# Hybrid decoder layer on one core: out-projection of four pairs of column tiles by seven products of blocks, and x added to the residual by adding transfers

## The chip, the cores and the metric

The kernel runs on one core of a Trainium2 chip. The metric is the device time of one execution in microseconds (us); a time given for a kernel is the median of its runs. The core's engines are PE (matrix products), DVE, ACT and POOL (elementwise work), and SP, which here issues nearly all transfers. Each engine works through its own instructions in order and waits for the others by semaphores.

## The reference

One decoder layer over 16 meta tokens and 512 tokens (528 positions), width 2048, all in float32:

```python
n = rmsnorm(h, g_pre_mix)
z = n @ w_in                                       # 2048 x 6592
y_conv = short_conv_group(z[..., :CONV_COLS], conv_w)
y_rwkv = rwkv7_group(z[..., CONV_COLS:], ...)      # a scan over the positions, 16 heads of 64
mix = concatenate([y_conv, y_rwkv], axis=-1) @ w_out   # 2048 x 2048, the out-projection
h = h + rmsnorm(mix, g_post_mix)                   # the first residual
f = conv_glu(rmsnorm(h, g_pre_ffn), w_gate_up, conv_ffn, w_down)   # FFN, 2048 -> 2 x 5632 -> 2048
h = h + rmsnorm(f, g_post_ffn)
return h[:, N_META:]
```

The change is in the line with `w_out` and in the first residual.

## The kernel before, in words

**Numbers.** Every float32 value is split into a high and a low part (ACT casts to get `hi`, DVE subtracts to get `lo`), and a product is three matmuls: hi by hi, hi by lo, lo by hi. Activations lie with the width on the partitions, in tiles of 128 rows by the positions; the 514 positions that are needed from the out-projection on are worked in two halves, `HY` = (0, 258) and (258, 514).

**Out-projection.** There are 16 column tiles `m` of 128 output rows. Each takes 4 weight blocks of 128x512 (`wload`: SP loads `raw`, which has 3 buffers; ACT casts `whi`, DVE subtracts `wlo`) and runs 16 row tiles k x 3 matmuls x 2 halves = 96 matmuls into one PSUM tile (`mps` or `u`). The 16 activation tiles `ys` are the outputs of the scan and of the convolution. Twelve of them come back from the DRAM tensor `ysp` through `r` and `v`, four are still on the chip, and all are split into `ahi` and `alo` just before the projection. `mixed` takes each result: ACT squares it (`q`), POOL adds the square into the sum `hxh` (the code's `ss`), and ACT copies it times a gain into `acc` (the code's `h`).

**Last two tiles, and the residual.** Column tiles 14 and 15 keep their split weights (`tt`), run half 0 of both and then half 1 of both, so that the norm and the residual of half 0 go beside the matmuls of half 1. The norm sums `hxh` and `q` over the partitions by matmuls with ones (`psn`) and ends in `r1p`. `residual(i)` then works through half i in 8 steps of two row tiles: DVE multiplies `acc` by `r1p`, x (which SP has loaded into a `raw` buffer) is added, by DVE and POOL in turn, and each row tile is split into activations for the FFN (`tt`, then `ahi` and `alo`). The second half also writes h to the DRAM tensor `hsp`.

**FFN.** The first two column blocks go by plain products, half 0 ahead of half 1. Later blocks go by `seven`: seven products of 2x2 blocks in place of eight, on sums of weight blocks and of activation blocks. Weights come as blocks `R` of 128x1024 (5 buffers); ACT casts `H`, DVE subtracts `O`.

**Order.** While `plan.on` holds, instructions are kept back, and a planner orders them with its own table of costs (0.42 us for an issue on SP, a latency for a landing, and so on). It is on from column tile `M0 = 10` to the end. Ahead of that, the order is the one in which the tile framework issues. All instructions that the planner has handled show one source line in the profile, L220, so that what follows goes by tile names.

```python
                (G if m % 4 else V).tensor_tensor(out=x, in0=x, in1=xr, op=ALU.add)
        for m in range(KT - 2):
            plan.on = m >= M0
```

Of the kernel before, what the change touches and what calls it, by code (L numbers as in the profile page):

```python
# [10 lines left out]
F32 = mybir.dt.float32  # L11
# [7 lines left out]
D = 2048  # L19
SEQ = 512  # L20
# [59 lines left out]

M0 = 10

# [141 lines left out]
class Plan:  # L224
# [3 lines left out]
    def __init__(self, tc):  # L228
        self.tc, self.on, self.kept, self.stage, self.rank, self.pe_rank = tc, False, [], 0, 2, 2

    @contextmanager
# [44 lines left out]
    def time(self, x):  # L276
# [46 lines left out]
    def land(self, x, issued):  # L323

        a = x["out"] if isinstance(x["out"], View) and x["out"].tile.pool.space != "dram" else x["ins"][0]
        n = a.parts * 4
        for s in a.ids.shape[1:]:
            n *= s
        self.pipe = max(self.pipe, issued) + n / 230e3
        return self.pipe + LAND + (2.0 if a.parts in (C, 4 * NC) else 0)  # L330

# [35 lines left out]
    def lag(self, u, v):  # L367

        e = self.engine[u]
        return 0.0 if e == self.engine[v] != "SP" else HOP[e]  # L370
# [44 lines left out]
    def run(self, rank):  # L415
# [10 lines left out]
        for _ in units:  # L426
# [31 lines left out]
            free[e], busy[e] = start + d, (start + d, self.two(x))  # L458
            end = self.land(x, start + d) if e == "SP" else start + d + (0.22 if e == "PE" else 0)
            for v in self.after[u]:  # L460
                o = self.engine[v]
                ready[v] = max(ready[v], start + d if o == e != "SP" else end + 0.07 + GAP[o])
# [17 lines left out]
def hymba(tc, I, out, ysp=None):  # L480
# [26 lines left out]
    if ysp is None:  # L507
        ysp = dp.tile([KT, 128, TY], F32, name="ysp")

    def wload(src, into=None):  # L510
# [27 lines left out]
    def run(g):  # L538
        for _ in g:
            pass  # L540
# [50 lines left out]
    with ExitStack() as ctx1:  # L591
# [455 lines left out]
        def head_norm(P, tags):  # L1047
# [41 lines left out]
            else:  # L1089
                o = p1.tile([128, LP], F32, name="k", bufs=2)[:, T0:L]  # L1090
                V.scalar_tensor_tensor(out=o, in0=yc[:, T0:], scalar=pc("lnb", P), in1=g[:, T0:], op0=ALU.add,
                                       op1=ALU.mult)
                ylast[NP + P] = o

        ylast = {}
        HC = ((T0 - 2, T0 - 2 + 258), (T0 + 256, L))

        def conv(j):
# [14 lines left out]
            (G if j < NP - 1 else V).tensor_tensor(out=u, in0=u, in1=zb, op=ALU.mult)  # L1113
            if j < NP - 1:
                SP.dma_start(ysp[j], u)
            else:
                ylast[j] = u
# [36 lines left out]
        while tasks or any(fills) or cur:  # L1154
# [32 lines left out]
            try:  # L1187
# [5 lines left out]
                cur = None  # L1193
        ys = []
        for i, k in enumerate(KORD):
            if k in ylast:
                yr = ylast[k]
            else:
                yr = p1.tile([128, LP], F32, name="rv"[i % 2], bufs=2)[:, :TY]
                SP.dma_start(yr, ysp[k])  # L1200
            hi, lo = a_tiles(i, TY)
            split(yr, hi, lo)
            ys.append((hi, lo))
        plan.give()


    with ExitStack() as ctx2:
# [42 lines left out]

        def mixed(ps, m, i):
            a, b = HY[i]
            x = ps[i][:, :b - a]
            sq[i] = ss[i] if m == 0 else small(b - a)
# [6 lines left out]
        def residual(i):  # L1261
# [26 lines left out]

        for m in range(KT - 2):
            plan.on = m >= M0  # L1290
            t = mp.tile([128, 2, 512], F32, name="mps")
            ps = [t[:, i] for i in range(2)]
            run(fill(gemm(I["w_out"][m], ys, [half(ps, i)[0] for i in range(2)])))
            for i in range(2):
                mixed(ps, m, i)

        H = KT // 2
# [3 lines left out]

        b11 = block(2)
        last = []
        for n, m in enumerate(range(KT - 2, KT)):
            kw = p2.tile([128, KT // 4, 2, 512], F32R, name=f"tt{n}", bufs=1)
            keep = [(kw[:, ku, 0], kw[:, ku, 1]) for ku in range(KT // 4)]
            if n == 0:
                ps = [ps2.tile([128, 512], F32, name="u", bufs=2) for _ in range(2)]  # L1310
            else:
                t = mp.tile([128, 2, 512], F32, name="mps")
                ps = [t[:, i] for i in range(2)]
            run(fill(gemm(I["w_out"][m], ys, half(ps, 0), into=keep)))
            mixed(ps, m, 0)
            last.append((ps, keep))
        n = 0
        res = iter(())
        for m, (ps, keep) in zip(range(KT - 2, KT), last):
            for _ in fill(gemm(None, ys, half(ps, 1), kept=keep)):  # L1320
                n += 1
                if n == N1:
                    rms1(0)
                    res = residual(0)
                if n % 4 == 0:
                    next(res, None)
            mixed(ps, m, 1)
        run(res)


        rb = wide("rb")
        rw = [rb[:, i * HW:i * HW + 258] for i in range(2)]

# [5 lines left out]
        def parted(raw, hi=None, lo=None):  # L1339
# [14 lines left out]
            return lambda c: at(hi, c), lambda c: at(lo, c)  # L1354

        def standard(outs, w, m0, x, first, last):
# [106 lines left out]

        def less(o, x, y):
            V.tensor_tensor(out=o, in0=x, in1=y, op=ALU.subtract)

        def sums(X2, X3):
# [68 lines left out]
        run(su)  # L1536


        X11 = [act(j, 0) for j in range(H)]
# [4 lines left out]
        X4 = [[x[:, :258] for x in hs[j]] for j in range(H)]  # L1544

        acc = p2.tile([128, KT, SEQ], F32, name="acc", bufs=1)

# [8 lines left out]
        def seven(f):  # L1556
# [15 lines left out]
            def plus(o, x, y):  # L1572
                V.tensor_tensor(out=o, in0=x, in1=y, op=ALU.add)

# [256 lines left out]
def layout(np, inp):  # L1831
# [20 lines left out]
    r["w_in"] = tiles(np.concatenate(cols, axis=1))  # L1852
    r["w_out"] = tiles(A["w_out"].reshape(KT, 128, D)[list(KORD)].reshape(D, D))

# [49 lines left out]
```

## Time and profile before

| | us |
|---|---|
| median of three runs (2397.4 to 2397.72) | 2397.53 |
| profiled execution, its own time | 2395.92 |
| its span, first to last instruction | 2394.1 |
| PE busy, 98% of the span | 2354.7 |
| DVE busy, 71% | 1699.1 |
| ACT busy, 50% | 1202.7 |
| POOL busy, 26% | 632.0 |

The mean granted TensorE clock was 0.996. The out-projection starts near 797 us and its last matmul is at about 981 us; the FFN follows. In tables by stretch, each line gives the stretch, its length, then the busy time and number of instructions of PE, PE's weight loads, DVE, ACT and POOL, then the granted clock, the busy share of the transfer engines, and GB/s. In tables of groups, each line has the count, the busy time and the mean in ns, and then the idle time before them with what ended it. In timelines, a line has the start, the duration, the instruction, and in brackets the idle time before it with its releaser.

### The profile page before, as it was taken

The numbers are of one execution on the slowest core, as the hardware profiler recorded it, in microseconds if no ns is written. First come the engines' busy times: TensorE is split into PE (matmuls) and PEld (weight loads), VectorE is DVE, ScalarE is ACT, GpSimd is POOL, SyncE is SP. The second block draws the span as 40 slices with busy tenths as digits, with TensorE's granted clock in tenths as the row PEclk, the third lists the DMA queues.
The fourth block names the chain that finished last, engine by engine and source line by source line (L and its number), as shares of the span: only waits on it lengthen the run. The fifth ranks groups of instructions, "written<-read, shape, count | busy, mean of one in ns | idle before, by whom it ended". The sixth has DMA issues, their size and how long they took to land.

```text
span 2394.1 us, 46253 instructions
## 1 busy us (share of the span) xinstructions
PE 2354.7 (98%) x18546; PEld 2249.2 (94%) x18546; DVE 1699.1 (71%) x2277; ACT 1202.7 (50%) x2364; POOL 632.0 (26%) x734
## 2 busy tenths in 40 slices
PE   7999999999999999999999999999999999999996
PEld 7999999999999999998999999999999998989896
DVE  7678888888764523785768677776868686859586
ACT  7766766767654434564434334343434342525254
POOL 2222646555451011210212121111212121202025
PEclk9999999999999999999999999999999999999998
DMA  5444333333432435523332324242324242423352
GB/s 178 151 132 121 89 92 89 105 107 95 130 103 85 133 93 176 177 76 106 96 116 80 124 80 133 80 124 81 123 74 130 71 134 79 124 88 107 96 191 71
DMA packets 130103, 265.53 MB, mean 111 GB/s; under 512 B 29888, under 2 KB 42944, under 8 KB 129888
## 3 DMA queue, kind: packets, MB, share of 16 engines
q1 hardware_dynamic: 129888, 262.57, 35.5%
q8 instruction: 146, 2.39, 0.4%
q14 instruction: 69, 0.57, 0.1%
HBM read 239.57 MB, written 22.95 MB: 110 GB/s over the span
## 4 chain that ended last, share of the span: by engine, by line
PE 56%; DVE 2%; issue 0%; ACT 0%; POOL 0%; ACTq 0%; DVEq 0%; POOLq 0%
PE mps L220 30%; PE u L220 16%; PE d L220 10%; DVE acc L220 1%; DVE alo L220 0%; DVE raw L220 0%; PE psn L220 0%; DVE q L220 0%; POOL raw L220 0%; ACT q L220 0%; DVE O L220 0%; DVE tt L220 0%; ACT raw L220 0%; ACT acc L220 0%; DVE r1p L220 0%
## 5 line engine op out<-in xcount | busy, mean ns | idle before, releaser
L220 ACT CAST H<-R 128x1024 fp32r<-128x1024 f32 x373 | 391.2, 1050 | 454.0 <-PE u L220 179.1
L220 DVE TENSOR_TENSOR O<-R,H 128x1024 fp32r<-128x1024 f32 x373 | 487.0, 1306 | 108.3 <-ACT H L220 107.5
L220 PE MATMUL mps<-ahi,whi 128*128 128x264 f32 (+2 forms) x2080 | 416.7, 288 | 10.5 <-ACT whi L220 10.5
L220 PE MATMUL mps<-alo,whi 128*128 128x264 f32 (+2 forms) x2080 | 416.0, 288 | 0.7 <-DVE alo L220 0.7
L220 PE MATMUL mps<-ahi,wlo 128*128 128x264 f32 (+2 forms) x2080 | 412.7, 287 | 1.6 <-DVE wlo L220 1.6
L220 DVE TENSOR_TENSOR wlo<-raw,whi 128x512 fp32r<-128x512 f32 x293 | 221.1, 758 | 208.1 <-ACT whi L220 189.0
L220 PEld LDWEIGHTS mps<-ahi,whi 128*128 128x128 f32 x2080 | 318.1, 189 | 13.2 <-ACT whi L220 10.7
L220 PEld LDWEIGHTS mps<-alo,whi 128*128 128x128 f32 x2080 | 317.6, 189 | 3.5 <-DVE alo L220 1.1
L220 PEld LDWEIGHTS mps<-ahi,wlo 128*128 128x128 f32 x2080 | 317.4, 190 | 3.8 <-DVE wlo L220 1.8
L220 ACT CAST whi<-raw 128x512 fp32r<-128x512 f32 x293 | 180.2, 619 | 195.9 <-PE mps L220 152.6
L220 POOL TENSOR_TENSOR raw<-raw,rb 128x516 f32<-128x516 f32 (+1 forms) x45 | 91.7, 2039 | 669.1 <-DVE raw L220 614.3
L220 PE MATMUL mps<-tt,H 128*128 128x258 f32 x1968 | 263.6, 284 | 1.3 <-DVE tt L220 1.3
L220 PE MATMUL mps<-alo,H 128*128 128x258 f32 x1032 | 253.7, 283 | 0.7 <-DVE alo L220 0.5
L220 PE MATMUL mps<-ahi,H 128*128 128x258 f32 x1032 | 253.4, 282 | 0.4 <-ACT ahi L220 0.4
L220 PEld LDWEIGHTS mps<-tt,H 128*128 128x128 f32 x1968 | 250.1, 189 | 2.4 <-DVE tt L220 1.6
L220 POOL TENSOR_TENSOR R<-R 128x1024 f32<-128x1024 f32 x40 | 131.4, 3286 | 422.6 <-DVE R L220 400.1
L220 DVE TENSOR_TENSOR R<-R 128x1024 f32<-128x1024 f32 x120 | 206.5, 1721 | 1.1
L220 PEld LDWEIGHTS mps<-ahi,H 128*128 128x128 f32 x1032 | 194.5, 190 | 0.6 <-ACT ahi L220 0.6
L220 PEld LDWEIGHTS mps<-alo,H 128*128 128x128 f32 x1032 | 193.9, 189 | 1.1 <-DVE alo L220 1.1
L220 POOL TENSOR_SCALAR SUV<-VT 32x64 f32<-32x64 f32 x272 | 138.0, 508 | 159.3 <-PE st L220 132.6
L220 PE MATMUL mps<-ahi,O 128*128 128x258 f32 x1032 | 152.5, 283 | 0.0
L220 PE MATMUL mps<-tt,O 128*128 128x258 f32 x984 | 141.1, 282 | 0.0
(318 smaller groups left out, 4409.1 us busy)
## 6 DMA issues: line engine op xcount, KB each, us to landing
R<-w_gu_dram SPq DMA_DIRECT2D x176, 512.0 KB, 3.6
raw<-w_in_dram SPq DMA_DIRECT2D x208, 256.0 KB, 2.7
R<-w_down_dram SPq DMA_DIRECT2D x88, 512.0 KB, 4.4
raw<-w_out_dram SPq DMA_DIRECT2D x64, 256.0 KB, 2.6
l<-lo SPq DMA_DIRECT2D x24, 264.0 KB, 2.3
hsp<-acc SPq DMA_DIRECT2D x8, 512.0 KB, 5.7
tt<-hsp SPq DMA_DIRECT2D x4, 1024.0 KB, 11.7
lo<-l SPq DMA_DIRECT2D x12, 264.0 KB, 2.8
```

The source lines that it names most:

```text
L220: return getattr(self.real, op)(*real, **{k: x.get() if isinstance(x, View) else x for k, x in kw.items()})
```

## The change

It has three parts.

**Seven products.** Column tiles 0 to 5 (`MS = 6`), 14 and 15 stay as they were. Tiles 6 to 13 become four pairs. A pair is a 2x2 arrangement of weight blocks (two row halves of 1024 by two columns of 128) against a 2x2 arrangement of activations (two row halves by the two halves of the positions). It takes 7 products of 8 row tiles x 3 matmuls of 258 columns. Its weights are four `R` blocks of 512 KB from a new tensor `w_pair`; DVE builds four sums of 128x1024 (`R<-R`) and the low parts of seven blocks. The sums of activations `T2`, `T3`, `T4` are built by `sums` during tiles 2 to 5 from 16 more reloads of `ysp`, and a fourth set, `Y1`, is written over half of the old activations by `again` (8 reloads). What it overwrites, half 1 of eight tiles, is written to a DRAM tensor `y12` ahead of that (16 writes of 128x256) and read back for tiles 14 and 15 (16 reads). Four `ylast` tiles are now also written to `ysp`.

**Residual.** SP's loads of x are gone, and so are the additions on POOL and DVE. POOL issues 16 transfers that add x from DRAM to `acc`.

**Order.** The planner is on from column tile 2 (`MP = 2`) and knows of transfers on POOL's queue: 0.9 us for the issue, 2.0 us more until it lands. `JS` sets how many `sums` stand ahead of which tile.

```diff
-M0 = 10
+MS = 6
+MP, JS, HEAD = 2, (0, 0, 3, 3, 2, 0), 8.0
...
         if e == "POOL":
+            if op == "dma_start":
+                return 0.9
...
+        return self.pipe + LAND + (2.0 if a.parts in (C, 4 * NC) or x["engine"].name == "POOL" else 0)
...
+        free["PE"] = self.head
...
             for m in range(0, KT, 2):
-                xr = wide().rearrange("p (m t) -> p m t", m=2)[:, :, :b - a]
-                SP.dma_start(xr, I["xT"][m:m + 2, :, T0 + a:T0 + b].rearrange("m p t -> p m t"))
-                x = h[:, m:m + 2, a:b]
+                x, src = h[:, m:m + 2, a:b], I["xT"][m:m + 2, :, T0 + a:T0 + b].rearrange("m p t -> p m t")
                 V.tensor_tensor(out=x, in0=x, in1=r1[i].unsqueeze(1).to_broadcast([128, 2, b - a]), op=ALU.mult)
-                (G if m % 4 else V).tensor_tensor(out=x, in0=x, in1=xr, op=ALU.add)
+                G.dma_start(x, src, accum_op=ALU.add)
...
+        def sums(j):
+            y = [big("R", F32)[:, :TY] for _ in range(2)]
+            for x, k in zip(y, (j, H + j)):
+                SP.dma_start(x, ysp[KORD[k]])
+            t = two()
+            less(t[:, 0], y[1][:, 256:], y[0][:, 256:])
+            plus(t[:, 1], t[:, 0], y[0][:, :258])
+            x = y[1][:, :258]
+            less(x, x, t[:, 1])
+            for o, x in ((T2, t[:, 1]), (T3, t[:, 0]), (T4, x)):
+                split(x, o[:, j, 0], o[:, j, 1])
...
-        for m in range(KT - 2):
-            plan.on = m >= M0
+        for m in range(MS):
+            plan.on = m >= MP
+            for _ in range(JS[m]):
+                sums(next(left))
...
+            if m == 1:
+                for x, o in zip(yf[:H], y12):
+                    for i in range(2):
+                        SP.dma_start(o[i], x[i][:, 258:TY].bitcast(F32))
...
+        for j in range(H):
+            y = again(j, wide()[:, :TY])
+            less(y[:, :258], y[:, 256:], y[:, :258])
+            split(y[:, :258], *[x[:, HA:HA + 258] for x in yf[j]])
...
+        def product(raw, x, o=None, start=True):
+            o = ps2.tile([128, 512], F32, name="u", bufs=2)[:, :258] if o is None else o
+            w = parted(raw)
+            for p, q in ((0, 0), (0, 1), (1, 0)):
+                with plan.step(2, FILL):
+                    for j in range(H):
+                        PE.matmul(o, w[p](128 * j), x[j][q], start=(start and p == q == j == 0), stop=p == 1 and j == H - 1,
+                                  skip_group_check=True)
+            return o
+
+        def pair(n):
+            a22, a21, a11, a12 = (load(I["w_pair"][n, i]) for i in (3, 2, 0, 1))
+            s1 = big("R", F32)
+            plus(s1, a21, a22)
+            k = two()
...
+            c = product(a11, Y11, mp.tile([128, 2, 512], F32, name="mps")[:, 0, :258])
+            S.copy(k[:, 0], c)
+            row(0, 0, product(a12, Y21), k[:, 0])
+            less(a11, s1, a11)
+            product(a11, Y2, c, False)
+            S.copy(k[:, 1], c)
+            less(a21, a22, a11)
+            less(a11, a12, a11)
+            plus(k[:, 1], product(a11, Y22), k[:, 1])
+            product(a21, Y3, c, False)
+            S.copy(k[:, 0], c)
+            product(a22, Y4, c, False)
+            row(1, 0, c)
+            o = product(s1, Y1)
+            row(0, 1, o, k[:, 1])
+            row(1, 1, o, k[:, 0])
+
+        for n in range((KT - 2 - MS) // 2):
+            pair(n)
...
+        for j in range(H):
+            for x, o in zip(yf[j], y12[j]):
+                SP.dma_start(x[:, 258:TY].bitcast(F32), o)
```

In program order, PE's matmuls go from 17593 to 17497: 384 of 256 columns leave and 288 of 258 columns are added. Three places in the order matter.

First, SP's queue at the start of the out-projection. Before, with `w_in` the end of the projection ahead, `w_out` the weights, and `r` and `v` the reloads of `ysp`:

```order
L220 DMA raw<-w_in_dram 128x512 x6
L220 DMA raw<-w_out_dram 128x512
L220 DMA r<-ysp 128x514
L220 DMA v<-ysp 128x514
L220 DMA r<-ysp 128x514
L220 DMA raw<-w_out_dram 128x512
L220 DMA v<-ysp 128x514
L220 DMA raw<-w_out_dram 128x512
L220 DMA r<-ysp 128x514
L220 DMA v<-ysp 128x514
```

And after:

```order
L223 DMA raw<-w_in_dram 128x512 x6
L223 DMA y_11765<-ahi_11275 128x256
L223 DMA raw<-w_out_dram 128x512
L223 DMA r<-ysp 128x514
L223 DMA y_11765<-alo_11287 128x256
L223 DMA v<-ysp 128x514
L223 DMA y_11765<-ahi_11291 128x256
L223 DMA y_11765<-alo_11301 128x256
L223 DMA r<-ysp 128x514
L223 DMA y_11765<-ahi_11309 128x256
L223 DMA raw<-w_out_dram 128x512
L223 DMA v<-ysp 128x514
```

The writes of `y12` now stand between the loads of the tiles and of the first weights; 13 of the 16 are ahead of the last `r`.

Second, POOL and DVE at the residual. POOL before:

```order
L220 TENSOR_TENSOR hxh<-hxh,q 128x258
L220 TENSOR_TENSOR acc<-acc,raw 128x2x258
L220 TENSOR_TENSOR hxh<-hxh,q 128x256
L220 TENSOR_TENSOR acc<-acc,raw 128x2x258 x3
L220 TENSOR_TENSOR acc<-acc,raw 128x2x256 x4
```

POOL after:

```order
L223 TENSOR_TENSOR hxh<-hxh,q 128x258
L223 DMA acc<-xT_dram 128x2x258 x2
L223 TENSOR_TENSOR hxh<-hxh,q 128x256
L223 DMA acc<-xT_dram 128x2x258 x6
L223 DMA acc<-xT_dram 128x2x256 x8
```

DVE after, from the norm of half 0 to the last multiplications of half 1:

```order
L223 TENSOR_TENSOR acc<-acc,r1p 128x2x258 x8
L223 TENSOR_TENSOR tt_13681<-R,tt_13681 128x1024 x2
L223 SCALAR_TENSOR_TENSOR tt_13738<-acc,par,tt_13738 128x258
L223 TENSOR_SCALAR q<-psn 128x256
L223 SCALAR_TENSOR_TENSOR tt_13738<-acc,par,tt_13738 128x258 x3
L223 TENSOR_TENSOR q<-q 128x256
L223 TENSOR_SCALAR q<-q 128x256
L223 TENSOR_TENSOR r1p<-hxl,q 128x256
L223 SCALAR_TENSOR_TENSOR tt_13738<-acc,par,tt_13738 128x258 x4
```

After these follow six low parts `alo` of half 0, three multiplications of half 1, two `alo` and the other five multiplications. Before, DVE's multiplications and additions alternated with the splits; now all eight multiplications of half 0 go first, and all additions are transfers on POOL's queue, half 1's behind half 0's.

Third, ACT at the start of the FFN, where `tt` with `acc` is the high part of an FFN activation and `q<-mps`, `acc<-mps` are the square and the copy of the last column tile's half 1. Before:

```order
L220 ACTIVATE q<-u 128x256
L220 CAST tt_13568<-R 128x1024
L220 ACTIVATE tt_13584<-acc,par 128x258 x2
L220 ACTIVATE acc<-u,par 128x256
L220 ACTIVATE tt_13584<-acc,par 128x258 x2
L220 CAST tt_13568<-R 128x1024
L220 ACTIVATE tt_13584<-acc,par 128x258
L220 ACTIVATE q<-mps 128x256
L220 ACTIVATE tt_13584<-acc,par 128x258
L220 ACTIVATE acc<-mps,par 128x256
```

After:

```order
L223 ACTIVATE q<-u 128x256
L223 CAST tt_13681<-R 128x1024 x2
L223 ACTIVATE acc<-u,par 128x256
L223 ACTIVATE q<-mps 128x256
L223 ACTIVATE acc<-mps,par 128x256
L223 ACTIVATE tt_13738<-acc,par 128x258 x4
L223 ACTIVATE hxl<-q 128x256
L223 ACTIVATE q<-hxl 128x256
L223 ACTIVATE tt_13738<-acc,par 128x258 x4
```

The six high parts that stood ahead of the last column tile's copy now stand behind it.

More of the change, by code (lines that the diff above doesn't have):

```diff
@@ L508, in hymba @@
         ysp = dp.tile([KT, 128, TY], F32, name="ysp")
+    y12 = dp.tile([KT // 2, 2, 128, 256], F32, name="y12")
     def wload(src, into=None):
@@ L1093, in head_norm @@
                 ylast[NP + P] = o
+                SP.dma_start(ysp[NP + P], o)
         ylast = {}
@@ L1302, in block, with plus, less @@
             return p2.tile([128, H, 2, 258], F32R, name=f"tt{n}", bufs=1)
[L1304 to L1332, printed above, removed]
+        def plus(o, x, y):
+            V.tensor_tensor(out=o, in0=x, in1=y, op=ALU.add)
+        def less(o, x, y):
+            V.tensor_tensor(out=o, in0=x, in1=y, op=ALU.subtract)
         def load(src):
@@ L1354, in parted @@
             return lambda c: at(hi, c), lambda c: at(lo, c)
+        T2, T3, T4 = (block(n) for n in range(3))
+        def sums(j):
[9 more added lines that the diff above has]
+                split(x, o[:, j, 0], o[:, j, 1])
@@ new lines, in hymba @@
+        left = iter(range(H))
+        plan.head = HEAD
+        for m in range(MS):
+            plan.on = m >= MP
+            for _ in range(JS[m]):
+                sums(next(left))
+            t = mp.tile([128, 2, 512], F32, name="mps")
+            ps = [t[:, i] for i in range(2)]
+            run(fill(gemm(I["w_out"][m], ys, [half(ps, i)[0] for i in range(2)])))
+            for i in range(2):
+                mixed(ps[i][:, :HY[i][1] - HY[i][0]], m, i)
+            if m == 1:
+                for x, o in zip(yf[:H], y12):
+                    for i in range(2):
+                        SP.dma_start(o[i], x[i][:, 258:TY].bitcast(F32))
@@ new lines, in hymba @@
+        for n in range((KT - 2 - MS) // 2):
+            pair(n)
+        b11 = block(2)
+        last = []
+        for n, m in enumerate(range(KT - 2, KT)):
+            kw = p2.tile([128, KT // 4, 2, 512], F32R, name=f"tt{n}", bufs=1)
+            keep = [(kw[:, ku, 0], kw[:, ku, 1]) for ku in range(KT // 4)]
+            if n == 0:
+                ps = [ps2.tile([128, 512], F32, name="u", bufs=2) for _ in range(2)]
+            else:
+                t = mp.tile([128, 2, 512], F32, name="mps")
+                ps = [t[:, i] for i in range(2)]
+            run(fill(gemm(I["w_out"][m - KT + 2 + MS], ys, half(ps, 0), into=keep)))
+            mixed(half(ps, 0)[0][0], m, 0)
+            last.append((ps, keep))
@@ new lines, in hymba @@
+        for j in range(H):
+            for x, o in zip(yf[j], y12[j]):
+                SP.dma_start(x[:, 258:TY].bitcast(F32), o)
+        n = 0
+        res = iter(())
+        for m, (ps, keep) in zip(range(KT - 2, KT), last):
+            for _ in fill(gemm(None, ys, half(ps, 1), kept=keep)):
+                n += 1
+                if n == N1:
+                    rms1(0)
+                    res = residual(0)
+                if n % 4 == 0:
+                    next(res, None)
+            mixed(half(ps, 1)[0][0], m, 1)
@@ L1356, in standard @@
+        run(res)
+        rb = wide("rb")
+        rw = [rb[:, i * HW:i * HW + 258] for i in range(2)]
         def standard(outs, w, m0, x, first, last):
@@ L1536, in hymba @@
         run(su)
+        acc = p2.tile([128, KT, SEQ], F32, name="acc", bufs=1)
         X11 = [act(j, 0) for j in range(H)]
```

56 lines of the change are left out of this document (32 added, 24 removed).

## Prediction

> **What bounds the kernel now.** I read the page first: the busy shares, then the chain that ended last.
>
> ```profile
> PE 2354.7 (98%) x18546; PEld 2249.2 (94%) x18546; DVE 1699.1 (71%) x2277; ACT 1202.7 (50%) x2364; POOL 632.0 (26%) x734
> ...
> PE 56%; DVE 2%; issue 0%; ACT 0%; POOL 0%; ACTq 0%; DVEq 0%; POOLq 0%
> ```
>
> PE is busy for 98% of the span and leads the chain: a matmul that leaves takes its time with it, provided that nothing else comes due at that place. So I read the windows next, one in the out-projection, one in the stage that already works by seven products, and those of the passage from the projection to the FFN.
>
> ```profile
> core 0: us, PE busy (x) PEld busy (x) DVE busy (x) ACT busy (x) POOL busy (x), PEclk, DMA share, GB/s
> 790.00:795.00 5.00, 5.00 (x44) 5.00 (x44) 5.00 (x7) 3.25 (x6) 0.89 (x1) 1.00 0.75 219
> 840.00:860.00 20.00, 20.00 (x168) 20.00 (x167) 4.85 (x7) 6.92 (x15) 2.99 (x4) 1.00 0.32 93
> 980.00:985.00 5.00, 3.61 (x25) 2.95 (x24) 4.67 (x9) 4.19 (x11) 2.53 (x2) 1.00 0.41 107
> 995.00:1000.00 5.00, 3.94 (x29) 3.32 (x27) 5.00 (x11) 3.33 (x8) 0.81 (x1) 1.00 0.84 271
> 1005.00:1010.00 5.00, 5.00 (x43) 5.00 (x43) 4.96 (x7) 2.94 (x6) 1.37 (x1) 1.00 1.03 383
> 1180.00:1200.00 20.00, 20.00 (x169) 20.00 (x168) 18.31 (x18) 10.32 (x14) 5.49 (x2) 1.00 0.35 106
> ```
>
> At 840 PE is full at 168 matmuls in 20.00 us, 0.119 us each, with DVE at a quarter. The seven-product stage at 1180 keeps PE full too, at the same pace, with DVE at 18.31 of 20. PE idles only at the passage: 1.39 us in 980 to 985 and 1.06 us in 995 to 1000. Its waits there are these:
>
> ```profile
> PE mps L220 <- DVE tt L220: 1.3, 1, 1.3
> PE mps L220 <- DVE alo L220: 0.5, 1, 0.5
> PE mps L220 <- ACT ahi L220: 0.4, 1, 0.4
> ```
>
> They end on the splits of FFN activations, that is, on the residual.
>
> **The matmuls.** 96 fewer stand in the order, and the clock stands at 1.00. 96 x 0.119 = 11.4 us, all on the engine that sets the end. (384 of 256 columns against 288 of 258, at 0.119 us for a mean of 257 columns, gives 11.1; I keep 11.4.) **-11.4.**
>
> **The start of the projection.** SP issues 16 writes of `y12` among the loads of tiles 0 and 1.
>
> ```profile
> 782.20 0.33 SPq L220 DMA_DIRECT2D raw<-w_out_dram  x1
> ...
> 791.47 0.32 SPq L220 DMA_DIRECT2D v<-ysp  x1
> 792.07 0.32 SPq L220 DMA_DIRECT2D r<-ysp  x1
> ...
> 795.82 0.33 SPq L220 DMA_DIRECT2D r<-ysp  x1
> 797.50 5.76 SPq L220 DMA_DIRECT2D raw<-w_out_dram  x3
> ```
>
> Issues that follow each other closely stand 0.60 us apart, so the 13 writes ahead of the last `r` take 7.8 us of the queue. Fourteen issues stand from 782.2 to the row at 797.5 today, 14 x 0.60 = 8.4 of 15.3 us, which leaves 6.9 us free. The other cushion is on DVE:
>
> ```profile
> 800.42 0.69 DVE L220 TENSOR_TENSOR alo<-r,ahi 128x514 fp32r<-128x514 f32 x1
> ...
> 970.62 0.43 DVE L220 TENSOR_SCALAR q<-psn 128x258 f32<-128x258 f32 x1 [11.60 <-PE psn L220]
> ```
>
> PE reaches the norm of half 0 at about 970; 1452 matmuls of the projection stand before it in the order, which puts the first at 970 - 172.8 = 797 and the block of rows 8 to 11, the first that needs the late tiles, 48 matmuls later, at about 803. The low part of the last `r` is there at 801.1: some 2 us of cushion. 7.8 - 6.9 = 0.9 is less than that, but each write also waits for its split, with the loads behind it waiting too. Transfers are busy 0.75 there, and 2.1 MB more (at 219 GB/s, 9.6 us) lie along some 20 us. I take **+0.5**, between 0 and 3 (7.8 - 6.9 and one reload's split late). The extra writes to `ysp` and the 16 reloads for `sums` lie in tiles 2 to 5, where transfers are at 0.32 and DVE at a quarter: nothing, since their 8 x 6 instructions on DVE, of 0.4 to 0.5 us (the rows of 258 columns below), are 21 us beside 45 us of matmuls; without the cover of a nearly idle DVE, the splits of tile 2's weights would be late by a `sums`, some 3 us.
>
> **The pairs.** What DVE does here is known from the seven-product stage:
>
> ```profile
> L220 DVE TENSOR_TENSOR O<-R,H 128x1024 fp32r<-128x1024 f32 x35 | 46.0, 1314 | 28.2 <-ACT H L220 28.0
> L220 DVE TENSOR_TENSOR R<-R 128x1024 f32<-128x1024 f32 x12 | 20.9, 1740 | 0.1
> ...
> L220 DVE TENSOR_TENSOR raw<-mps,q 128x258 f32<-128x258 f32 x4 | 1.7, 420 | 0.3 <-PE mps L220 0.3
> ```
>
> And on the page, ACT's share of the same:
>
> ```profile
> L220 ACT CAST H<-R 128x1024 fp32r<-128x1024 f32 x373 | 391.2, 1050 | 454.0 <-PE u L220 179.1
> ```
>
> A pair has seven low parts, 7 x 1.31 = 9.2, four sums, 4 x 1.74 = 7.0, four small additions, 1.7, and a fourth of `again`'s 16 small ones, 1.7: 19.6 us, against 168 x 0.119 = 20.0 on PE. That is as tight as the window at 1180, which loses nothing. ACT has 7 x 1.05 us and some copies and squares, half of its time. Each pair's four loads (2.1 MB in 20 us, 105 GB/s) are what that window moves. Five `R` buffers hold four blocks and `s1`, so a pair's loads wait until the pair before has split its last blocks. I take **+0.5**; the bounds are 0 and one sum uncovered per pair, 4 x 1.74 = +7.0.
>
> **The read-back of `y12`.** 16 reads begin when the last s1 product has gone; tile 14's and 15's half 0 cover them, some 114 matmuls or 13.5 us, for 16 x 0.60 = 9.6 us of issues. Nothing; without cover, what lands late is late for half 1.
>
> **The start of the FFN.** ACT first:
>
> ```profile
> 977.60 0.91 ACT L220 ACTIVATE tt<-acc,par 128x258 fp32r<-128x258 f32 x2
> ...
> 980.96 0.38 ACT L220 ACTIVATE q<-mps 128x256 f32<-128x256 f32 x1 [0.78 <-PE mps L220]
> ...
> 981.64 0.47 ACT L220 ACTIVATE acc<-mps,par 128x256 f32<-128x256 f32 x1
> ```
>
> DVE's multiplications of half 0, and the low part that PE waits for:
>
> ```profile
> 973.32 2.50 DVE L220 TENSOR_TENSOR acc<-acc,r1p 128x516 f32<-128x516 f32 x4
> ...
> 983.07 1.14 DVE L220 SCALAR_TENSOR_TENSOR tt<-acc,par,tt 128x258 fp32r<-128x258 f32 x1
> ```
>
> PE's first matmuls of the FFN:
>
> ```profile
> 981.74 0.59 PE L220 MATMUL mps<-tt,H 128*128 128x258 f32 x2
> ...
> 984.27 0.39 PE L220 MATMUL mps<-tt,H 128*128 128x258 f32 x1 [1.35 <-DVE tt L220]
> ```
>
> Now no high part stands ahead of the copy, which can follow the square at 981.34 and ends at 981.75; the first high part is there at about 982.2 and its low part at 982.6, each taking 0.4 to 0.5 us (the first row; two took 0.91). PE, ready at 981.74, waits 0.45 and 0.28, in place of 1.39: **-0.7.** All eight multiplications of half 0 are done by 973.32 + 8 x 0.62 = 978.3, so x has some 4 us to be added in.
>
> **The second half of the residual.** DVE does no additions any more, so its multiplications of half 1 start behind ten low parts of half 0 (22 took 9.6, so 10 x 0.43), counted from `r1p`:
>
> ```profile
> 985.07 0.43 DVE L220 TENSOR_TENSOR r1p<-hxl,q 128x256 f32<-128x256 f32 x1
> ```
>
> The low part's own price, POOL's addition of x, its last addition to `hxh`, and what such transfers take to land:
>
> ```profile
> L220 DVE SCALAR_TENSOR_TENSOR alo<-acc,par,ahi 128x258 fp32r<-128x258 f32 x22 | 9.6, 491 | 0.0
> ```
>
> ```profile
> L220 POOL TENSOR_TENSOR acc<-acc,raw 128x516 f32<-128x516 f32 x4 | 5.1, 1300 | 16.8 <-DVE acc L220 10.1 <-DMA raw<-xT_dram 6.7
> ```
>
> ```profile
> 975.74 1.18 POOL L220 TENSOR_TENSOR hxh<-hxh,q 128x256 f32<-128x256 f32 x1 [0.34 <-ACT q L220]
> ```
>
> ```profile
> hsp<-acc SPq DMA_DIRECT2D x8, 512.0 KB, 5.7
> ...
> raw<-xT_dram SPq DMA_DIRECT2D x8, 258.0 KB, 3.6
> ```
>
> That is 985.5 + 4.3 + one multiplication of 0.6, and 0.8 for waits on ACT and on x: about 991.2. PE's first matmul on half 1 stands 135 behind the first of the FFN, 982.4 + 16.1 = 998.5, and that on the last two row tiles 111 later, at 1011.7. No adding transfer is in the trace. Its landing I put at 5.7, the `hsp` row, which moves twice the bytes, since what is added to has to be read as well; the plain load's 3.6 is the lower end. First step: 991.2 + 5.7 + 1.0 for the splits = 997.9, in time. Last step: 991.2 + 5.7 + 7g + 1.0 against 1011.7, where g is the pace at which these transfers follow each other: in time up to g = 1.97. The lower end of g is SP's issue pace, 0.60 (POOL's own addition, which it replaces, took 1.30), and the upper a queue on which each waits until the one before has landed, 3.6. I take the middle, 2.1: last step 0.9 late. Today's 1.06 I leave, since its splits stay. **+0.9**, from -1.06 (all on time) to what the third rival gives. Behind a late transfer wait, on DVE, the low parts of half 0, then the multiplications of half 1; on POOL, `raw<-raw,rb` of the FFN; on SP, the eight `hsp` writes, while transfers are full (1.03) at 1005.
>
> At this place a rule of the Trainium skill bears. "Collectives: The Full Stack", section "The bandwidth ceiling: the fold count and why AG ≠ RS ≠ AR", says that an add in a transfer needs two source reads and so twice the reading per byte. By it and the window's 383 GB/s, an estimate, each 0.26 MB costs 1.4 us rather than 0.7; at g = 1.4 the last step would be on time, the term 0 and the time 2386.4 instead of 2387.3. No run here shows it yet.
>
> **Sum.** -11.4 + 0.5 + 0.5 - 0.7 + 0.9 = -10.2, against the profiled execution's own 2395.92 (its span of 2394.1 and 1.8 around it). That one was 1.6 below the median of 2397.53; against the median, **2387.3 us**.
>
> **Rivals.** *The pairs are bound by DVE.* For it: 19.6 of 20.0 with five buffers, and one sum that is late each time shows on PE at once. Against: the window at 1180. One sum per pair: 7.0 in place of 0.5, 2393.8.
>
> *Adding transfers at a middling pace.* POOL's queue holds 14 of the 16 behind its addition to `hxh` that ends near 976.9 (975.74 + 1.18). Above g = 2.4 this queue sets the end: the last lands at 976.9 + 13g + 5.7 against 1010.7, so 13g - 28.1 us of idling. At g = 2.4 to 3.4 that is 3.1 to 16.1 in place of the 1.06: 2388.4 to 2401.4.
>
> *They go one at a time* (slower than before). At g = 3.6 the idling is 18.7, +17.6 where I have +0.9: 2404.0. It decides from 13g - 28.1 - 1.06 = 16 on, g = 3.5. For it: no row shows transfers on POOL's queue overlapping, since it has none. Against: SP's overlap, 0.60 apart with landings of 3.6.
>
> The Trainium skill speaks for this rival: "SBUF — State Buffer", section "SBUF: two separate sides", with the subsection "A bandwidth-pool intuition that's wrong (but worth ruling out)", says that POOL writes the descriptors of its transfers itself and is locked out while DVE runs an op in a two-port mode, 620 ns becoming 3100. By this figure, g = 3.1 and 2397.5, no change; but it names copies and casts for such modes, and the rows of DVE here are of two tensor operands.
>
> **How the numbers follow.** The forecast has 0.65 (2383.5 to 2390.5), the DVE-bound pairs 0.13, the middling pace 0.14, one at a time 0.08. 0.2% is 4.8 us, about what a measurement of this kernel can tell from no change. Faster, below 2392.7: the forecast, half of the middling pace (to g = 2.7) and some of the pairs, 0.77. Within: the rest of both, 0.15. Slower: 0.08. The range: from 2383.5, where nothing idles but at the first start (-11.4 - 0.7 - 1.06 and 0.8 for the rest), to 2394.5, which takes in the pairs and the middling pace to g = 2.8.
>
> **What the profile of the changed kernel would show.** PE with 96 matmuls fewer and windows of 20.00 in the pairs; idling there that ends on `O` or `R` means the pairs are dearer. Idling near 787 to 805 that ends on `alo` means SP's queue. The wait on `tt` at the passage is shorter than 1.35. The rows of `acc<-xT_dram` give g: below 2.1 the second half is on time, above 3.5 the kernel is slower. What would make me wrong most is that pace, which nothing here shows.

## Result and profile after

The changed kernel takes 2451.71 us (median of 6, 2448.97 to 2455.04), the kernel before 2397.53: 1.0226 times the time, interval 1.0213 to 1.0239. That is 54 us slower, where 10 us faster was forecast. The profiled execution took 2448.97 (span 2447.2), 53.05 more than that of before.

The page and its chain:

```profile
PE 2375.2 (97%) x18450; PEld 2253.0 (92%) x18450; DVE 1755.9 (72%) x2361; ACT 1228.2 (50%) x2404; POOL 647.5 (26%) x742
...
PE 89%; issue 3%; DVE 3%; DMA 2%; ACT 2%; POOL 1%; SPq 0%; ACTq 0%; POOLq 0%; DVEq 0%
```

PE has its 96 matmuls fewer (18450 for 18546) and is busy 20 us longer. Two new entries stand in the chain, transfers (DMA 2%) and "issue", time in which an engine waits for nothing that the profile shows. The windows show where (same columns as in the prediction):

```profile
900.00:920.00 20.00, 20.00 (x168) 20.00 (x167) 14.34 (x16) 11.29 (x18) 4.43 (x4) 1.00 0.33 104
...
960.00:980.00 20.00, 17.17 (x126) 15.64 (x125) 12.02 (x22) 6.67 (x14) 4.50 (x4) 1.00 0.48 96
980.00:1000.00 20.00, 10.06 (x39) 8.07 (x39) 3.55 (x8) 4.13 (x10) 5.07 (x5) 0.58 0.40 53
1000.00:1020.00 20.00, 13.56 (x87) 12.27 (x87) 9.38 (x17) 5.58 (x11) 4.68 (x4) 0.84 0.59 120
1020.00:1040.00 20.00, 9.73 (x34) 7.90 (x35) 4.64 (x10) 5.08 (x11) 4.87 (x4) 0.50 0.65 148
1040.00:1060.00 20.00, 16.73 (x94) 15.88 (x93) 12.31 (x20) 11.96 (x22) 1.22 (x1) 0.72 0.48 114
```

In the pairs (900) PE is full. From 960 to 1060 it is busy for 67.3 of 100 us, and for half of that stretch the granted clock is down to 0.50. No engine is near its limit there, and transfers are not either (0.40 to 0.65). POOL's own timeline names the cause; a line has start, duration, instruction, and the idle time before it with what ended it:

```profile
990.03 1.22 POOL L223 DMA_DIRECT2D acc<-xT_dram  x1 [3.51 <-issue]
994.96 1.21 POOL L223 DMA_DIRECT2D acc<-xT_dram  x1 [3.71 <-issue]
999.81 1.22 POOL L223 DMA_DIRECT2D acc<-xT_dram  x1 [3.64 <-issue]
```

ACT, which splits what has landed, in the same stretch:

```profile
994.66 0.91 ACT L223 ACTIVATE ahi<-acc,par 128x258 fp32r<-128x258 f32 x2 [4.02 <-DMA acc<-xT_dram]
999.52 0.91 ACT L223 ACTIVATE ahi<-acc,par 128x258 fp32r<-128x258 f32 x2 [3.94 <-DMA acc<-xT_dram]
```

And the summary of the transfers by their tile:

```profile
L223 POOL DMA_DIRECT2D acc<-xT_dram x16: 1204/1222/1390, 964.8 to 1045.0; - x16
...
  ACT ahi L223: 48.5, 12
  ACT tt L223: 9.3, 3
...
DMA to landing us min/median/max: 4.3/5.1/6.6
```

A transfer lands (ACT starts at 994.66), and 0.3 us later POOL issues the next (994.96). Never are two under way: in the trace each of the other 15 is issued only after the last packet of the one before. The 13 steps from the third issue at 975.46 to the last at 1044.97 are 5.35 us each, and ACT waited 58 us for them.

The trace can be split at marks that both executions have. The matmuls of the first norm (`psn<-hxh`) and of the last (`psn<-raw`), first and last start, before and after:

```profile
L220 PE MATMUL psn<-hxh,ones x4: 377/380/383, 969.5 to 981.0; 128*128 128x258 f32 x2, 128*128 128x256 f32 x2
...
L220 PE MATMUL psn<-raw,ones x12: 377/379/483, 1020.9 to 2374.4; 128*128 128x256 f32 x8, 128*128 128x258 f32 x4
```

```profile
L223 PE MATMUL psn<-raw,ones x12: 377/379/483, 1060.7 to 2427.6; 128*128 128x256 f32 x8, 128*128 128x258 f32 x4
...
L223 PE MATMUL psn<-hxh,ones x4: 378/379/484, 959.9 to 971.9; 128*128 128x258 f32 x2, 128*128 128x256 f32 x2
```

One output of the seven-product stage, the eighth `raw<-mps,q` on DVE in both executions, before and after:

```profile
1198.37 0.42 DVE L220 TENSOR_TENSOR raw<-mps,q 128x256 f32<-128x256 f32 x1 [1.23 <-PE mps L220]
```

```profile
1240.58 0.42 DVE L223 TENSOR_TENSOR raw<-mps,q 128x256 f32<-128x256 f32 x1 [1.22 <-PE mps L223]
```

At the end of the projection the changed kernel is 9.1 us ahead (971.9 for 981.0). At 1198 it is 42.2 behind: the passage cost 51.3. At the end it is 53.2 behind: 11.0 more went in the rest of the FFN, where PE is full in both and the order is the same. That last part the prediction had not thought of. It is in the matmuls of 512 columns of the down projection, here those of whi with H into `d` between 1200 and 2200, before and then after (busy, mean ns of one):

```profile
L220 PE MATMUL d<-whi,H 128*128 128x512 f32 x192 | 74.7, 389 | 0.0
```

```profile
L223 PE MATMUL d<-whi,H 128*128 128x512 f32 x192 | 75.6, 394 | 0.0
```

From start to start such a matmul takes 227 ns before and 228 to 241 after (232 in the mean). 1920 of them stand in the program: 1920 x 5.5 ns = 10.6 us. The two programs differ in what these matmuls read: with the new tiles `tt` asked for earlier, the split weights H, O and the activation hxl have moved from 150880, 163168 and 208480 bytes of a partition to 200416, 212704 and 224992.

### The profile page after: what moved, and what is told of

Same layout as the page of the kernel before. It is cut to its first block, busy times and chain, and to the rows that moved or that the text cites. A ratio compares the mean times of both kernels' runs of the same rounds, so it can differ in the third digit from the quotient of the medians.

```text
span 2447.2 us, 46249 instructions
## 1 busy us (share of the span) xinstructions
PE 2375.2 (97%) x18450; PEld 2253.0 (92%) x18450; DVE 1755.9 (72%) x2361; ACT 1228.2 (50%) x2404; POOL 647.5 (26%) x742
## 3 DMA queue, kind: packets, MB, share of 16 engines
q0 software_dynamic: 4352, 4.21, 1.3%
## 4 chain that ended last, share of the span: by engine, by line
PE 89%; issue 3%; DVE 3%; DMA 2%; ACT 2%; POOL 1%; SPq 0%; ACTq 0%; POOLq 0%; DVEq 0%
PE mps L223 56%; PE u L223 17%; PE d L223 10%; PE st L223 4%; PE aux L223 2%; DVE acc L223 1%; POOL acc L223 1%; DMA acc<-xT_dram 0%; DMA R<-w_down_dram 0%; DMA l<-lo 0%; DVE raw L223 0%; DMA k<-xT_dram 0%; DMA d<-tb 0%; DVE O L223 0%; DVE alo L223 0%
## 5 line engine op out<-in xcount | busy, mean ns | idle before, releaser
L223 ACT CAST H<-R 128x1024 fp32r<-128x1024 f32 x401 | 419.2, 1047 | 492.7 <-PE u L223 187.0
L223 DVE TENSOR_TENSOR O<-R,H 128x1024 fp32r<-128x1024 f32 x401 | 521.9, 1302 | 126.6 <-ACT H L223 119.5
L223 PE MATMUL mps<-ahi,whi 128*128 128x264 f32 (+2 forms) x1824 | 365.1, 289 | 10.6 <-ACT whi L223 10.6
L223 PE MATMUL mps<-alo,whi 128*128 128x264 f32 (+2 forms) x1824 | 364.3, 289 | 0.9 <-DVE alo L223 0.9
L223 PE MATMUL mps<-ahi,wlo 128*128 128x264 f32 (+2 forms) x1824 | 361.5, 288 | 1.6 <-DVE wlo L223 1.6
L223 PE MATMUL mps<-tt,H 128*128 128x258 f32 x2160 | 290.2, 284 | 7.5 <-ACT tt L223 6.2
L223 PEld LDWEIGHTS mps<-ahi,whi 128*128 128x128 f32 x1824 | 278.6, 189 | 13.2 <-ACT whi L223 10.8
L223 PEld LDWEIGHTS mps<-tt,H 128*128 128x128 f32 x2160 | 273.5, 190 | 10.5 <-ACT tt L223 7.2
L223 PEld LDWEIGHTS mps<-alo,whi 128*128 128x128 f32 x1824 | 278.0, 189 | 3.5 <-DVE alo L223 1.1
L223 PEld LDWEIGHTS mps<-ahi,wlo 128*128 128x128 f32 x1824 | 277.5, 190 | 3.8 <-DVE wlo L223 1.8
```

Of the source, the lines that this page charges most:

```text
L223: return getattr(self.real, op)(*real, **{k: x.get() if isinstance(x, View) else x for k, x in kw.items()})
```

## The experiments

Two theories stood after this. First: adding transfers on POOL's queue go one at a time, and that is the loss in the passage; rivals, that the pairs or POOL's queue as such are at fault. Second: the place of H, O and hxl makes the down projection slow; rival, that it follows from the transfers or from the dropped clock. Each run's median stands beside that of the kernel before in the same runs, with the ratio's interval.

**1. x loaded by SP, added by DVE and POOL.** The pairs and the order stay.

```diff
+                xr = wide().rearrange("p (m t) -> p m t", m=2)[:, :, :b - a]
+                SP.dma_start(xr, I["xT"][m:m + 2, :, T0 + a:T0 + b].rearrange("m p t -> p m t"))
...
-                G.dma_start(x, src, accum_op=ALU.add)
+                (G if m % 4 else V).tensor_tensor(out=x, in0=x, in1=xr, op=ALU.add)
```

> The changed kernel with x loaded by SP and added by DVE and POOL, as in the kernel before; the seven products and the order stay. Theory: the adding transfers, which go one at a time, cost the 51 us between the norm of half 1 (9.1 us earlier than before) and the seven-product stage (42.2 us later), idle PE and halved clock together; here the passage is like the kernel before's and the clock stays 1.00. The rest of the loss, 0.14 us on each group of 24 matmuls of 512 columns in the down projection (5.44 to 5.58 us, some 11 us in all), is put down to where the weight blocks H and O lie: it then stays, and the time is 2397.5 - 9.1 + 11 = about 2399. Rival: that part too comes with the adding transfers, and the time is about 2388. Rival to both: the pairs are at fault, and it stays above 2440.

2402.37 beside 2398.76, ratio 1.0007 to 1.0026. 49 us are gone with the adding transfers, and the slow matmuls stayed: 232 ns, and a lead of 4.8 us near 1150 that turned into 5.8 us behind near 2300. Both theories hold, and the pairs are cleared. The 3 us above the expected 2399 lie in the passage: PE idles 5.0 us between 960 and 1000, where it idled 2.45 before.

**2. The same, with H and O at the places of before.** Six copies of one column at the first `sums` make the program give them those places.

```diff
+            if j == 0:
+                for t in ("H", "O"):
+                    for _ in range(3):
+                        V.tensor_copy(out=big(t).bitcast(F32)[:, :1], in_=y[0][:, :1])
```

> As the run without adding transfers, and H and O at the addresses that they have in the kernel before (six copies of one column ahead of the first sums, so that they are placed there). If the place of H and O makes the down projection's matmuls slow: 5.44 us per group of 24 again, and about 2388. If it is something else that the change brings: 5.58 and as the run without this edit.

2388.77 beside 2398.76, 0.9940 to 0.9974: 13.6 us less than run 1. Only the products with hxl, left at 224992, stayed slow:

```profile
L223 PE MATMUL d<-whi,H 128*128 128x512 f32 x192 | 74.7, 389 | 0.0
...
L223 PE MATMUL d<-hxl,H 128*128 128x512 f32 x64 | 25.3, 395 | 0.0
```

So the place matters for the moving operand too (the 512 columns that stream past the weights, here hxl), and the dropped clock isn't the reason.

**3. The kernel before with the adding transfers alone.** The edit of the residual and the planner's costs for it; no pairs.

> The kernel before with the adding transfers alone (and the planner's costs for them): no pairs, planner from column tile 10. Theory: 16 transfers one at a time, 5.0 us apart or more, clock at half in stretches near 985 to 1060: 2397.5 + 51 = about 2449, and the down projection's groups at 5.44. Rival (the slow matmuls of the down projection come with the adding transfers): about 2460. Rival (it is the pairs together with the transfers): within 10 us of 2397.5.

2441.94 beside 2398.76, 1.0167 to 1.0197: 43 us, 8 less than the 51 expected, with matmuls at 227 ns. The transfers go one at a time here as well, 5.29 us apart. What is less is the time at the low clock: over the 110 us of the passage the granted clock was 0.81 in the mean (970 to 1080), against 0.75 in the changed kernel (960 to 1070): 0.06 x 110 is some 7 us of clock.

**4. Plain transfers on POOL's queue.** Run 1 with x loaded by `G.dma_start`, all additions on DVE.

> The changed kernel with x loaded into raw by plain transfers on POOL's queue, added by DVE. If POOL's queue takes one transfer at a time whatever it does: issues follow each landing, 3 to 5 us apart, and the time stays above 2430. If only adding makes them wait for each other: two or three are under way at once (raw has three buffers), and the time is that of the run with x loaded by SP, within 5 us.

2399.23 beside 2398.76, 0.9995 to 1.0013. Plain transfers on this queue overlap:

```profile
978.90 1.45 POOL L223 DMA_DIRECT2D raw<-xT_dram  x2 [2.94 <-DVE acc L223]
...
987.00 1.45 POOL L223 DMA_DIRECT2D raw<-xT_dram  x2 [1.82 <-DVE acc L223]
```

Two follow each other within 0.72 us, while none lands in under 3.2, and the waits end on DVE, which frees the buffers. POOL's queue as such is cleared. What differs in an adding transfer shows in the queue's totals, of this run and then of the changed kernel:

```profile
q0 software_dynamic: 1280, 4.21, 0.6%
```

```profile
q0 software_dynamic: 4352, 4.21, 1.3%
```

For the same 4.21 MB there are 3.4 times the packets, 272 a transfer for 80 (in the trace 256 of 1032 or 1024 bytes and 16 of 4, for 64 of 4128 or 4096 and 16 of 4), and an issue takes POOL 1.22 us for 0.72.

**5. The place alone, in the kernel before.** One column each of acc, q, R and the `tt` blocks is set to zero ahead of the projection, so that H, O and hxl come to lie where the changed kernel has them.

> The kernel before, with nothing of the change, only that acc, q, R and the tt blocks get their places first (one column of each set to zero ahead of the projection), so that H, O and hxl lie where the changed kernel has them (from 200416, 212704 and 224992 bytes of a partition on, in place of 150880, 163168 and 208480). If the place makes the matmuls of 512 columns slow: 232 ns each in place of 227, 5.58 us per group of 24, and 2397.5 + 12 = about 2410. If it takes the pairs too: within 1 us of the kernel before.

2408.26 beside 2397.51, 1.0026 to 1.0059: 10.75 us from the places of tiles alone, with nothing else of the change.

```profile
L220 PE MATMUL d<-whi,H 128*128 128x512 f32 x192 | 75.6, 394 | 0.0
```

**6. Only H moved down,** to 183904; O and hxl stay. This is run 1 with `T3` split ahead of `T2` and the six copies of run 2 behind the first split.

> The changed kernel without adding transfers (x loaded by SP), with H alone moved down, to 183904 to 196191; O and hxl stay high. If weights read from the high places are slow wherever they are used: groups with H at 227 ns, those with O at 229 to 241, with hxl 234, and about 2392. If O's or hxl's place alone decides: all stay at 232 and the time at 2402.

2398.97 beside 2397.51, 0.9997 to 1.0015. Neither case: products with H were mixed, from 224 ns (one of the three `whi` buffers) to 237, those with O 229 to 233, hxl 234. "High is slow" does not describe it.

**7. Adding transfers in halves,** one row tile each, 32 in place of 16.

```diff
-                G.dma_start(x, src, accum_op=ALU.add)
+                for n in range(2):
+                    G.dma_start(x[:, n], src[:, n], accum_op=ALU.add)
```

> The changed kernel with each adding transfer in two, one row tile each: 32 of 128x258. If the room of POOL's queue for work under way decides (one transfer of 264 KB and not two): two or more halves are under way at once, the pace for a pair of row tiles falls from 5.3 to about 3 us, and the time to about 2425. If adding transfers wait for each other whatever their size: each half takes its own 3 to 4 us, a pair 7, and the time rises to about 2480.

2410.37 beside 2397.51, 1.0039 to 1.0069: 41 us less than the changed kernel, more than the 27 expected.

```profile
993.19 2.68 POOL L223 DMA_DIRECT2D acc<-xT_dram  x3 [2.69 <-issue]
...
DMA to landing us min/median/max: 3.0/4.7/8.1
```

Three are issued within 2.7 us, before the first can have landed; then POOL waits. From 966.9 on there are 29 steps in 47.9 us, 3.3 for a pair of row tiles. So adding transfers do not wait for each other as such: the queue holds a limited amount of them, one of 264 KB or three of 132; in the traces of this run and of run 12 never more than three of the 32 are under way. A limit in bytes does not fit run 4, where by the packets three plain transfers of 264 KB, 792 KB, were under way at 990.5. A limit in packets would: 144 a half (4608 in all for 32), so 432 were held, while two whole transfers would be 544. That packets are what is counted is not shown: the queue's room (`dynamic_dma_scratch_size=1024` in every kernel here) was not varied.

**8. Plain transfers, with H, O and hxl low** (152960 to 177535), by the copies of run 2 with hxl ahead of them.

> The seven products with x loaded by plain transfers on POOL's queue and added by DVE, and with H, O and hxl at low places (152960 to 177535). If place and adding transfers are the whole of the loss: the run with plain transfers (2399) less 13, about 2386, under the kernel before by 11 to 13 us; matmuls of 512 columns all at 227 ns. If something of the pairs is left: above 2390.

2401.47 beside 2397.51, 1.0007 to 1.0026: a miss of 15 us. All products were slow, at 231 to 235 ns, with every operand at a low place:

```profile
L223 PE MATMUL d<-whi,H 128*128 128x512 f32 x192 | 75.9, 395 | 0.0
```

What had been moved, besides, was the remainder modulo 512: H and O stand at 352 in the kernel before, at 224 in the changed one, at 384 here; whi, wlo and hxh at 96 throughout.

**9. Plain transfers, every tile at exactly the place of before.** The same zeroing as in run 5, in the old order.

> The seven products with x loaded by plain transfers on POOL's queue and added by DVE, and every tile of this stage at exactly the place that it has in the kernel before (one column of each set to zero by POOL ahead of the projection, in that order). If adding transfers and place are the whole of the loss: matmuls of 512 columns at 227 ns throughout, 2399 - 12 = 2387, under the kernel before. If a low place alone had been wanted, the run with both edits would have had it already; then this one stays near 2400.

2388.80 beside 2398.12, 0.9946 to 0.9973. 227 ns throughout, and faster than before.

**10. The change as made, with the places of before.**

> The changed kernel as it is, adding transfers and all, with the tiles at the places of the kernel before. Place theory: 227 ns for 512 columns and 2451.7 - 12 = about 2440, that is, the two causes add up. If the slow matmuls hang on the idle stretches or the halved clock as well: above 2446.

2441.06 beside 2398.12, 1.0162 to 1.0189. The two causes add up: the place is 10.7 us here (from 2451.71), and the adding transfers are 52.3 (2441.06 less run 9).

**11. Run 4 with 128 bytes left free ahead of H,** at the changed kernel's own high places.

```diff
+        for n in ["hxh", "acc", *["q"] * 3, *["R"] * 5, "1", "0", "2", "pad"]:
+            t = (first[n] if n in first else two()[:, 0] if n == "q" else big(n).bitcast(F32) if n in WB
+                 else p2.tile([128, 32], F32, name=n, bufs=1) if n == "pad" else tt[int(n)][:, 0, 0].bitcast(F32))
+            G.memset(t[:, :1], 0.0)
```

The tiles ahead of H are asked for in the changed kernel's order, by one zeroed column each; `pad` is the 128 bytes. H comes to 200544, O to 212832, hxl to 225120.

> As the run with plain transfers on POOL's queue, at the changed kernel's own high places, but with 128 bytes of a partition left free ahead of H, so that H and O stand at 352 modulo 512 as in the kernel before (the moving operands whi, wlo and hxh stand at 96). If the place counts modulo 512, 256 apart being the good case: products with whi, wlo and hxh at 227 ns, those with hxl slow, and 2399 - 10 = about 2389. If high places are slow, or the pattern is another: 231 to 233 ns as before and about 2399.

2385.82 beside 2398.12, 0.9934 to 0.9961: 13.4 us from 128 bytes (run 4 was 2399.23), and the fastest of all. Even hxl, expected slow, is fast:

```profile
L223 PE MATMUL d<-whi,H 128*128 128x512 f32 x192 | 74.7, 389 | 0.0
...
L223 PE MATMUL d<-hxl,H 128*128 128x512 f32 x64 | 24.9, 389 | 0.0
```

**12. Adding transfers in halves, places of before.**

> The changed kernel with adding transfers in halves and the tiles at the places of the kernel before: 2410.4 - 12 = about 2398, the kernel before's time; three halves under way at once still set a pace of 3 us for a pair of row tiles. If the half transfers gain from the quicker stage too: below 2394.

2397.17 beside 2398.12, 0.9989 to 1.0007, as expected: what the pairs gain, the half transfers take back (8.4 us against run 9).

## Why the prediction was wrong

**The step that failed first is the second half of the residual, +0.9 us in the sum.** Its pace g, put at 2.1 us a transfer, was 5.35. In place of this term and of the -0.7 for the start of the FFN stand 51.3 us in the trace (and 52.3 between runs 10 and 9). The prediction had named that pace as what would make it wrong most. The mechanism was there as the third rival, "one at a time", at a chance of 0.08; its size was wrong as well, +17.6. Three things went into that:

- The pace g of a queue that takes one at a time was put at 3.6, the landing of a plain load, while the same paragraph put the landing of an adding transfer at 5.7. One at a time means one landing each: by its own 5.7 the rival's formula gives 13 x 5.7 - 28.1 = 46 us, and 2431. Measured were landings of 5.1 in the median and g = 5.35, for which the formula gives 41.5 us of idling; PE idled 32.8.
- The low clock had no price. By the windows above, PE idled 32.8 us between 960 and 1060, 30.3 more than the 2.45 of before; the rest of the 51.3, some 21 us, is matmuls at a lower clock: the 380 matmuls of these windows are busy for 67.3 us, and at the 0.119 us each of a full window they would take 45.2. The windows' means of 0.58, 0.84, 0.50 and 0.72 come to 54 of the 100 us at 0.50. The Trainium skill, "TensorE: Matmul & The Clock Gate", section "What's actually happening" of Part 1, says that the array falls to half its clock after an idle window of about 3.4 us. In the trace it took less: the granted clock is 0.50 from 983.1 to 1003.4, and it fell there 0.7 us into a wait of 3.2, the longest of the passage so far, after one of 2.4 (the lines below). PE was busy for 11.8 of these 20.3 us. The waits of 1.39 and 1.06 us in the kernel before left the clock at 1.00.
- The first half was thought safe, with "some 4 us to be added in". At 5 us each its eight transfers hold the queue until 1005, and PE's first waits end on `tt`, half 0:

```profile
975.79 0.91 PE L223 MATMUL mps<-tt,H 128*128 128x258 f32 x2 [0.65 <-ACT tt L223]
...
980.61 0.91 PE L223 MATMUL mps<-tt,H 128*128 128x258 f32 x2 [2.36 <-ACT tt L223]
...
985.57 1.10 PE L223 MATMUL mps<-tt,H 128*128 128x258 f32 x2 [3.22 <-ACT tt L223]
```

What spoke against the rival, that SP's transfers overlap, was a fact about plain transfers on another queue. Run 4 shows that plain ones overlap on POOL's queue too; run 7, that the amount of work under way is what counts. No row of the kernel before had an adding transfer, so the range had to hold its whole unknown, and the chance of 0.08 had nothing behind it.

The reason for this rival that the prediction took from the Trainium skill, "SBUF — State Buffer", section "SBUF: two separate sides", descriptor writing that a busy DVE locks out, is not the one here: DVE was busy for 3.55 of 20 us in the window from 980 to 1000, where the transfers were 5 us apart.

**The second failure is a term that was missing:** the place of tiles that the change does not name. It cost 10.7 us (runs 5 and 10) and would by itself have taken the whole gain. The order of PE's last 9143 matmuls, from the start of the seven-product stage to the end, is the same in both traces; the addresses that they read are not.

**What held.** The matmuls, the start of the projection and the pairs were -11.4 + 0.5 + 0.5 = -10.4. The trace has the projection 9.1 us ahead at its end after starting about 1.1 late (the last `z<-mps` of the input projection starts at 797.2 for 796.0), so -10.2. SP's 16 writes among the loads cost nothing: PE was full from 780 to 880. One wait of 0.9 us (on `q`) stands between 890 and 895 in place of the 0.5 that I gave to the pairs. DVE was far from bounding them: its row here, O<-R,H and R<-R between 900 and 960, is

```profile
L223 DVE TENSOR_TENSOR O<-R,H 128x1024 fp32r<-128x1024 f32 x18 | 22.5, 1252 | 13.7 <-ACT H L223 8.3 <-PE mps L223 5.1
L223 DVE TENSOR_TENSOR R<-R 128x1024 f32<-128x1024 f32 x8 | 9.9, 1237 | 0.5 <-DMA R<-w_pair_dram 0.3
```

A sum takes 1.24 us here in place of the 1.74 taken from a stage in which POOL adds blocks as well; DVE had 14.3 us in the window at 900. The first rival was therefore never near. **The start of the FFN** (-0.7) can't be read from the changed kernel, whose first splits waited for transfers; in runs 9 and 11, with x added by DVE, the wait there is 1.2 us on `tt`.

With both causes removed, runs 9 and 11 are 9.3 and 12.3 us faster than the kernel before in the same runs, where 10.2 was forecast for the whole. They load x by plain transfers and let DVE add it, so that this is near to what the pairs are worth, not a measure of them alone; and of the 12.3 some 2.8 are again the place, as the next paragraph shows.

**What stays open:** why the place matters. The good cases have H and O at 352 modulo 512 beside moving operands at 96; those at 224 and 384 were slow throughout, H at 96 was mixed, and hxl was slow at 224 (run 2) and fast at 352 (run 11), both beside an H at 352. That is a pattern of few points. Which part of the address decides was not settled, nor why matmuls of 258 columns show it so little: the 6048 of them between the first and the last matmul of 512 columns take 120.24 ns each before and in run 9, 120.43 in the changed kernel and 119.78 in run 11. That last step is still 2.8 us, which is about what run 11 is faster than run 9.

## What to carry to other kernels

A kind of transfer that the trace has never shown has no upper bound in the rows of another kind: put "one at a time" at the full landing, multiply it by the count, and add what an idling PE loses in clock; then either give that case a real chance or measure it first. An edit that asks for tiles in another order moves all tiles behind it: compare the addresses of what the hot matmuls read, as one compares the order, and try a small pad. When a change does two things, run them apart; here the kernels with the pairs and without the two causes were 9 to 12 us faster than before, and the adding transfers cost 52.

## What the hardware showed that I had not expected

- Adding transfers on POOL's queue: one of 264 KB under way at a time, or three of 132 KB; 272 packets where a plain one has 80; 1.22 us of issue for 0.72; 5.1 us to land where plain ones on the same queue took 4.0.
- A matmul of 512 columns took from 224 to 241 ns, start to start, by the place of its weights and its moving operand alone, steadily for a given place. 128 bytes between two tiles were worth 13 us of 2400.
